# A fused attention, gate and embedding layer: where the last sums and reloads stand at the seam into the gate product

## The chip, the cores and the metric

The kernel runs on one core of a Trainium2 chip. The metric is the device time of one execution in microseconds (us), here the median of several runs. All times below that are not called runs come from one profiled execution.

## The reference

One layer, for a sequence of 1024 positions and a width of 1024, all in float32:

```python
h = rms_norm(x, mix_norm_g)
dq, dk, dv, bq, bk, bv, z = split(h @ w_in)
A = diff_attention(...)      # 4 heads, difference of two softmaxes, ALiBi, norm of each head
B = dilated_attention(...)   # 8 heads, three window patterns merged by their denominators
x = x + (concat[A, B] * silu(z)) @ w_out
gate = sigmoid(rms_norm(x, ple_norm_g) @ w_ple_gate)
x = x + gate * (p @ w_ple_proj)
```

## The kernel before

Everything is computed transposed, with features on the 128 partitions. Each float32 operand of a large product is cut into a rounded part "hi" and a rest "lo": ScalarE (ACT) casts the hi part, VectorE (DVE) or GpSimd (POOL) subtracts it to get the lo part, and TensorE (PE) does three matmuls (hi·hi, hi·lo, lo·hi) for each block of 128 features. Unless said otherwise a tile is 128x512.

The program has stages that follow each other on PE: the first projections, the dilated attention, the differential attention with the z product woven in, the product with `w_o`, and at the end the product with the gate weights `w_g` and the embedding. Two seams matter here.

**Seam 1, the end of the differential attention** (`step(g)`, g from 30 to 35). For each pair of query blocks `values` accumulates in a PSUM tile `od`, ACT squares it, and `sums` adds the squares over the partitions with four small matmuls into a PSUM tile `pss`, which DVE copies to `ssq` (L1202). `od` and `pss` are made in the same PSUM pool. `factors(3, 0, 4, V)` turns the first four sums of the last head into scale factors: a chain of small 128x4 instructions on DVE (tiles `dtmp`, `dfac`: L104, L106, then three rounds of L113, L115, L117, then L1237). It is a generator, and `bit(n)` issues the next n of its pieces where `step` calls it. `z_part(n)` issues the next n matmuls of the z and `w_o` products (`pso`), which fill PE between the parts of the attention.

**Seam 2, from the `w_o` product into the gate product.** The gate product of two feature blocks at once uses seven products of sums and differences (a Strassen-Winograd scheme): with the four quarters of `x1` (11, 21, 22 and a sum) and three more sums t2, t3, t4 of them on one side, and the weights' quarters with their sums s1, s2, s4 on the other. `sums_x1(3)` makes the last t2, t3, t4 on DVE (tiles `xe`, `xd`), each cut into hi and lo (`bt`). `w_gate(i)` loads the weights of step i, makes their sums on POOL and cuts all seven; step 0's are made ahead, those of step i+1 within step i. In the loop over i, `m(ps, w, k)` is one of the seven products (12 matmuls), and `taken` copies a PSUM tile to SBUF on ACT (L1624): `p1`, `p5`, `u2`, `u3`. The products "22", "t2", "t3" and "t4" accumulate into PSUM tiles that have been copied before, so each of them waits for such a copy. `norm2` sums the squares of `x1` with 16 matmuls of one column (tile `pm`) and ends in a broadcast reload `rb2`. `emb_product` is the embedding's product (6 matmuls, PSUM tile `psp`), from weights `wpr` and inputs `p` that `emb_w` and `emb_in` load and cut. `out_gate` scales, takes the sigmoid through tanh, multiplies, adds `x1` (reloaded from HBM by `x1_in` on ACT's DMA queue) and stores.

In seam 1 the order on PE, DVE, ACT, POOL and SP is the order of the code. From the end of the first `w_o` blocks on (`MAN4 = "PG"`) it is so for PE and POOL alone; DVE, ACT and SP follow a scheduler's list. Every engine works through its own list in order, and a DMA issue that waits for a buffer holds what stands behind it on its queue, on ACT the compute too.

Of the kernel before, what the change touches and what calls it, by code (L numbers as in the profile page):

```python
# [18 lines left out]
P = 128  # L19
# [55 lines left out]
def tile_hybrid_layer(ctx: ExitStack, tc, xT, w_att, w_z, w_o, w_g, w_p, pT, vec, lamv, tdil, tdiff, outT):  # L75
# [704 lines left out]
    with ExitStack() as pb:  # L780
# [528 lines left out]
        def step(g):  # L1309
            k = g // 2  # L1310
            zp_ = ZP[0], ZP[1] + (g % 3 == 0)
            if g >= 31:
                zp_ = ZT[g - 31]
            in_slot()
            scores(g + 1, 0)
            bit(BITS)
            z_part(zp_[0])
            exps(g + 1, 0)
            combine(g)
            bit(BITS)  # L1320
            turn(g - 1, 0)
            turn(g - 1, 1)
            if g % 2:
                sums(k - 2)
                if g in (11, 19, 27):
                    small_ops.append(factors((g - 11) // 8))
                elif g == 31:
                    small_ops.append(factors(3, 0, 4, V))
                elif g == 35:
                    for _ in factors(3, 4, 8, V):  # L1330
                        pass
            scores(g + 1, 1)
            turn_lo(g - 1, 0)
            turn_lo(g - 1, 1)
            if g < 32:
                bit(BITS)
            if g % 2:
                if 26 < g < 32:
                    z_part(zp_[1])
                values(k - 1, 0)  # L1340
            else:
                values(k - 2, 1)
            if g > 31:
                in_slot()
                bit(BITS)
            bit(BITS)
            if g < 32:
                fetch(g)
            if g % 2 == 0 or not 26 < g < 32:
                z_part(zp_[1])  # L1350
            if g in Y_IN:
                y_diff_in(*Y_IN[g])
            if g - 1 in Y_IN:
                y_diff(*Y_IN[g - 1])
            if g in (32, 33):
                y_split(6, g - 32, ga[2, g - 32][0])
            if g == 33:
                bit(100)
                G.tensor_mul(heads["a"][:, 0:512], heads["a"][:, 0:512], last_z[0])
            if g == 34:  # L1360
                y_last(0)
            bit(BITS)
            exps(g + 1, 1)
# [20 lines left out]
    with ExitStack() as pc:  # L1384
# [15 lines left out]
        def p_tile(shape, name):  # L1400
            return ps_t.tile(shape, F32, tag="t", name=name)

        def stage(name, src, q=nc.sync):
            t = inp.tile([P, 512], F32, tag="in", bufs=4, name=name)
            q.dma_start(t, src)
            return t
# [76 lines left out]

        def sums_x1(i):

            e, d = X[2 * i, "e"], X[2 * i, "d"]
            V.scalar_tensor_tensor(out=e, in0=X[2 * i + 1, 1], scalar=g2(2 * i + 1), in1=e, op0=ALU.mult, op1=ALU.subtract)
            V.scalar_tensor_tensor(out=d, in0=X[2 * i, 0], scalar=g2(2 * i), in1=e, op0=ALU.mult, op1=ALU.add)
            cut("t2", i, d)
            cut("t3", i, e)  # L1490
            V.scalar_tensor_tensor(out=d, in0=X[2 * i + 1, 0], scalar=g2(2 * i + 1), in1=d, op0=ALU.mult, op1=ALU.subtract)
            cut("t4", i, d)
# [42 lines left out]
        def emb_w(n):  # L1535
            hi, lo = wp[n] = [h_tile(f"wp{k}_{n}").rearrange("p (f a c) -> p f a c", f=4, a=2) for k in ("hi", "lo")]
            for b in range(2):
                fs = slice(2 * b, 2 * b + 2)
                raw = stage(f"wpr_{n}_{b}", w_p[n][:, fs].rearrange("p f a c -> p (f a c)"))
                split(hi[:, fs], lo[:, fs], raw.rearrange("p (f a c) -> p f a c", f=2, a=2))  # L1540
# [10 lines left out]
        def w_gate(i):  # L1551
# [9 lines left out]
            t = {1: q11, 5: s1, 2: q12, 6: s2, 7: q21, 3: s4, 4: q22}  # L1561
            return {n: w_cut(t[n], f"m{n}_{i}", G if i == 1 and n in (1, 5, 6) else V) for n in ORDER[i > 0]}

# [4 lines left out]
        out(7, 1)  # L1568
        sums_x1(3)
        first = h_tile("p15").bitcast(F32)  # L1570
# [24 lines left out]
        def g_tile(name):  # L1595
            return gp.tile([P, 512], F32, tag="g", bufs=6, name=name)

        pls = {}

# [14 lines left out]
        def x1_in(f, half):  # L1614
            t = gp.tile([P, 512], F32, tag="x", bufs=2, name=f"x1b_{f}_{half}")
            A.dma_start(t, x1_d[f, :, half * 512 : half * 512 + 512])
            return t
# [11 lines left out]
        for i in range(4):  # L1629
# [6 lines left out]
            first = []  # L1636
            if after:
                after.pop(0)()
            if i == 0:
# [3 lines left out]
                V.tensor_add(p1, p1, pb_)  # L1643
                m(pc_, w[3], "22", **more)
                emb_w(0)
                emb_in(0)
                emb_in(1)
                w_next = w_gate(1)
            m(pa_, w[6], "t2", **more)
            u2 = taken(f"u2_{i}", pa_)  # L1650
            if i:
                m(pb_, w[2], "21")
                V.tensor_add(p1, p1, pb_)
# [16 lines left out]
            else:  # L1670
                m(pa_, w[7], "t3", **more)
            u3 = taken(f"u3_{i}", pa_)
            if i == 0:
                emb_product(f0, 1)
                out_gate(f0, 0, p1, p1, x1_in(f0, 0))
                out_gate(f0, 1, u2, u2, x1_in(f0, 1))
            elif i < 3:
                w_next = w_gate(i + 1)
            G.tensor_add(u3, u3, p5)

# [106 lines left out]
```

## Time and profile before

| what | us |
|---|---|
| median of 3 runs (825.5 to 828.95) | 825.77 |
| the profiled execution's own time | 826.21 |
| its span, first to last instruction | 824.4 |
| PE busy in the span | 804.6 |
| DVE busy | 594.4 |
| ACT busy | 484.7 |
| POOL busy | 393.0 |
| mean granted clock of PE | 0.993 of full |

A granted clock of 1.00 is PE's upper level, 2.4 GHz; 0.50 is its lower level, 1.2 GHz. A matmul's row gives its start and a duration that runs into the next one's, so the pace of a stretch is read from the starts.

### The profile page before, as it was taken

How to read it: one execution, taken by the hardware profiler on the slowest of the kernel's cores; microseconds unless marked ns; L12 is line 12 of the kernel's file. 1: busy time of each engine (PE TensorE's matmuls, PEld its weight loads, DVE VectorE, ACT ScalarE, POOL GpSimd, SP SyncE). 2: the span in 40 equal slices, each digit the busy share in tenths (PEclk: the TensorE clock that was granted, in tenths of full speed). 3: DMA queues.
4: the chain of work that ended last, by engine and by line, in shares of the span. 5: the costliest groups of instructions: out<-in, count | busy, mean ns of one | idle time of the engine just before them, and what ended most of it. 6: DMA issues, size and time to landing. Idle time of an engine off the chain costs nothing.

```text
span 824.4 us, 13381 instructions
## 1 busy us (share of the span) xinstructions
PE 804.6 (98%) x4328; PEld 685.1 (83%) x4328; DVE 594.4 (72%) x1307; ACT 484.7 (59%) x1000; POOL 393.0 (48%) x432
## 2 busy tenths in 40 slices
PE   9999999999999999999999999999999999989997
PEld 8888888888788888887788888888887888868886
DVE  6948544566977687765788787888864598776773
ACT  8553423366866696665687877886771355443331
POOL 5602110226672665122367898885562343744552
PEclk9999999999999999999999999999999999989999
DMA  7621679465878579897487683944591453443422
GB/s 270 203 65 52 187 218 305 156 158 141 239 214 243 136 244 270 250 271 199 131 227 192 180 256 116 268 128 161 191 401 40 158 175 102 154 142 130 137 81 98
DMA packets 114773, 150.22 MB, mean 182 GB/s; under 512 B 11264, under 2 KB 70288, under 8 KB 114704
## 3 DMA queue, kind: packets, MB, share of 16 engines
q1 hardware_dynamic: 111680, 144.00, 57.7%
q10 hardware_dynamic: 3024, 5.38, 2.1%
q8 instruction: 34, 0.56, 0.3%
q14 instruction: 35, 0.29, 0.1%
HBM read 101.95 MB, written 47.39 MB: 181 GB/s over the span
## 4 chain that ended last, share of the span: by engine, by line
PE 80%; DVE 8%; issue 4%; POOL 4%; ACT 3%; DMA 1%; DVEq 0%; ACTq 0%; POOLq 0%
PE mm L256 5%; PE mm L258 5%; PE mm L257 5%; PE mm L508 5%; PE mm L512 5%; PE mm L510 5%; PE s L598 3%; PE psz L960 2%; PE psz L962 2%; PE psz L958 2%; PE sd L1114 2%; PE pso L1430 2%; PE pso L1428 2%; PE pso L1429 2%; PE sd L1115 2%
## 5 line engine op out<-in xcount | busy, mean ns | idle before, releaser
L1138 POOL TENSOR_TENSOR ed<-ed,ed 128x512 f32<-128x512 f32 x64 | 81.6, 1298 | 49.7 <-ACT ed L1136 44.3
L1126 ACT ACTIVATE ed<-ed,nm 128x1024 f32<-128x1024 f32 x64 | 73.8, 1153 | 47.0 <-DVE nm L1117 47.0
L627 ACT ACTIVATE e<-e,stats 128x256 f32<-128x256 f32 x128 | 64.8, 508 | 33.9 <-DVE stats L618 33.4
L510 PE MATMUL mm<-w2l,h_hi 128*128 128x512 f32 x192 | 78.9, 411 | 0.0
L508 PE MATMUL mm<-w2h,h_hi 128*128 128x512 f32 x192 | 78.6, 409 | 0.0
L512 PE MATMUL mm<-w2h,h_lo 128*128 128x512 f32 x192 | 76.0, 396 | 0.0
L257 PE MATMUL mm<-wl,h_hi 128*128 128x512 f32 x192 | 75.3, 392 | 0.0
L258 PE MATMUL mm<-wh,h_lo 128*128 128x512 f32 x192 | 75.1, 391 | 0.0
L256 PE MATMUL mm<-wh,h_hi 128*128 128x512 f32 x192 | 74.1, 392 | 0.0
L618 DVE CUSTOM_DVE_ANT_0 e<-s,tb 128x256 f32<-128x256 f32 x128 | 49.0, 418 | 20.3 <-PE s L598 19.6
L656 DVE TENSOR_TENSOR pl<-t,ph 128x512 fp32r<-128x512 f32 (+2 forms) x72 | 45.2, 628 | 19.1 <-ACT ph L651 17.0
L1117 DVE CUSTOM_DVE_ANT_0 ed<-sd,td,nm 128x512 f32<-128x512 f32 x64 | 48.1, 751 | 11.0 <-PE sd L1115 1.5
L1117 DVE CUSTOM_DVE_ANT_0 ed<-sd,td 128x512 f32<-128x512 f32 x64 | 43.9, 686 | 16.6 <-PE sd L1115 15.4
L1114 PE MATMUL sd<-kh,qs 128*128 128x512 f32 x128 | 53.4, 417 | 1.1 <-DVE nm L1117 0.6
L651 ACT CAST ph<-t 128x512 fp32r<-128x512 f32 (+2 forms) x72 | 38.2, 532 | 23.3 <-PE t L638 11.5
L1159 DVE TENSOR_TENSOR pld<-td,phd 128x512 fp32r<-128x512 f32 x64 | 42.0, 687 | 12.5 <-ACT phd L1150 12.1
L1115 PE MATMUL sd<-kl,qs 128*128 128x512 f32 x128 | 50.1, 392 | 0.0
L958 PE MATMUL psz<-h_hi,zhi 128*128 128x512 f32 x128 | 50.1, 392 | 0.0
L960 PE MATMUL psz<-h_lo,zhi 128*128 128x512 f32 x128 | 50.1, 392 | 0.0
L962 PE MATMUL psz<-h_hi,zlo 128*128 128x512 f32 x128 | 50.1, 391 | 0.0
L432 POOL TENSOR_TENSOR sq<-raw 128x512 f32<-128x512 f32 x16 | 17.1, 1070 | 63.4 <-ACT raw L430 61.1
L257 PEld LDWEIGHTS mm<-wl,h_hi 128*128 128x128 f32 x192 | 36.1, 188 | 7.4
(341 smaller groups left out, 2491.6 us busy)
## 6 DMA issues: line engine op xcount, KB each, us to landing
kn<-bk_d SPq DMA_DIRECT2D x16, 512.0 KB, 7.6
w2r<-in_w_att_dram SPq DMA_DIRECT2D x24, 256.0 KB, 4.3
y<-yd_d SPq DMA_DIRECT2D x12, 512.0 KB, 7.3
x<-in_xT_dram SPq DMA_DIRECT2D x16, 256.0 KB, 5.4
wr<-in_w_att_dram SPq DMA_DIRECT2D x8, 512.0 KB, 4.6
qn<-bq_d SPq DMA_DIRECT2D x16, 256.0 KB, 5.1
bv_d<-bv SPq DMA_DIRECT2D x16, 256.0 KB, 4.1
vc<-bv_d SPq DMA_DIRECT2D x32, 128.0 KB, 4.4
```

Source lines behind the costliest of these rows:

```text
L256: T.matmul(ps, h_hi[d][:, ts_], wh, start=(d == 0), stop=False)
L257: T.matmul(ps, h_hi[d][:, ts_], wl, start=False, stop=False)
L258: T.matmul(ps, h_lo[d][:, ts_], wh, start=False, stop=(d == 7))
L508: T.matmul(ps, h_hi[d][:, ts_], wh, start=(d == 0), stop=False)
L510: T.matmul(ps, h_hi[d][:, ts_], wl, start=False, stop=False)
L512: T.matmul(ps, h_lo[d][:, ts_], wh, start=False, stop=(d == 7))
L958: T.matmul(ps, hi, h_hi[d][:, hs], start=(d == 0), stop=False)
L960: T.matmul(ps, hi, h_lo[d][:, hs], start=False, stop=False)
L1114: T.matmul(ps, q, kh[:, c, hs], start=True, stop=False)
L1117: V.tensor_tensor_reduce(out=sp[:, hs], in0=ps, in1=td[:, off : off + 512], scale=4.0 ** -(hd + 1), scalar=BIG if half == 0 else nm[:, 0:1 ...
L1126: A.activation(sp, sp, AF.Exp, bias=nm[:, 1:2], scale=-1.0, accum_out=l)
L1138: G.tensor_add(w[:, hs], w[:, hs], e1[:, hs])
```

## The change

`step` no longer issues pieces of the factors' chain from g = 32 on; the remaining ones all come at g = 33, behind the copy of the row sums. At g = 33 three of the second half's z-path matmuls are taken ahead of `values`. In seam 2 the third sum of `sums_x1(3)` (t4) is split off as `sum_t4` and issued after "22". `w_gate(1)` is called behind `u3`'s copy and the sum `u3 + p5`; in the later steps that sum moves ahead of `w_gate(i + 1)`. The lo cuts of `w_gate(1)`'s products 1, 5 and 6 go from POOL to DVE. The reloads of `x1` use the four "in" buffers except for the first feature block, and the second embedding weights use the two "x" buffers. The postponed second embedding product of step 0 and the last one of each later step move one product on.

```diff
-            bit(BITS)
+            n_bits = BITS if g < 32 else 0
+            bit(n_bits)
...
                 sums(k - 2)
+                if g == 33:
+                    bit(10)
...
             if g % 2:
-                if 26 < g < 32:
-                    z_part(zp_[1])
+                if 26 < g < 34:
+                    z_part(zp_[1] if g < 32 else 3)
                 values(k - 1, 0)
...
-                z_part(zp_[1])
+                z_part(zp_[1] - 3 * (g == 33))
...
-        def sums_x1(i):
+        def sums_x1(i, late=False):
...
+            if not late:
+                sum_t4(i)
+
+        def sum_t4(i):
+            d = X[2 * i, "d"]
             V.scalar_tensor_tensor(out=d, in0=X[2 * i + 1, 0], scalar=g2(2 * i + 1), in1=d, op0=ALU.mult, op1=ALU.subtract)
             cut("t4", i, d)
...
-                raw = stage(f"wpr_{n}_{b}", w_p[n][:, fs].rearrange("p f a c -> p (f a c)"))
+                raw = (x_tile if n else in_tile)(f"wpr_{n}_{b}")
+                nc.sync.dma_start(raw, w_p[n][:, fs].rearrange("p f a c -> p (f a c)"))
...
-            return {n: w_cut(t[n], f"m{n}_{i}", G if i == 1 and n in (1, 5, 6) else V) for n in ORDER[i > 0]}
+            return {n: w_cut(t[n], f"m{n}_{i}") for n in ORDER[i > 0]}
...
-        sums_x1(3)
+        sums_x1(3, late=True)
...
-            t = gp.tile([P, 512], F32, tag="x", bufs=2, name=f"x1b_{f}_{half}")
+            t = (in_tile if f else x_tile)(f"x1b_{f}_{half}")
...
-            if after:
-                after.pop(0)()
...
                 m(pc_, w[3], "22", **more)
+                sum_t4(3)
                 emb_w(0)
                 emb_in(0)
                 emb_in(1)
-                w_next = w_gate(1)
...
             if i:
+                if len(after) > 1:
+                    after.pop(0)()
                 m(pb_, w[2], "21")
...
             u3 = taken(f"u3_{i}", pa_)
+            G.tensor_add(u3, u3, p5)
             if i == 0:
+                w_next = w_gate(1)
...
-            G.tensor_add(u3, u3, p5)
```

On DVE at seam 1 the chain of factors stands, before the change, ahead of the copy of the row sums (`ssq_6896<-pss`) and partly ahead of the cuts `pld` and the product `asb`:

```order
L113 TENSOR_TENSOR dtmp_0_7702<-dfac_0_7701 128x4
L115 SCALAR_TENSOR_TENSOR dtmp_0_7702<-dtmp_0_7702,sub_6897 128x4
L1159 TENSOR_TENSOR pld_0_7655<-td_0_7721,phd_0_7654 128x4x128
L1159 TENSOR_TENSOR pld_1_7663<-td_1_7727,phd_1_7662 128x4x128
L1185 TENSOR_TENSOR asb_7422<-od_7686,zt_1_7633 128x256
L117 SCALAR_TENSOR_TENSOR dfac_0_7701<-dtmp_0_7702,dfac_0_7701 128x4
L113 TENSOR_TENSOR dtmp_0_7702<-dfac_0_7701 128x4
L115 SCALAR_TENSOR_TENSOR dtmp_0_7702<-dtmp_0_7702,sub_6897 128x4
L117 SCALAR_TENSOR_TENSOR dfac_0_7701<-dtmp_0_7702,dfac_0_7701 128x4
L1270 TENSOR_TENSOR y_0_7762<-ya_0_7538,y_0_7762 128x512
L1237 TENSOR_SCALAR dfac_0_7701<-dfac_0_7701 128x4
L1202 COPY ssq_6896<-pss_7778 128x2
```

and after it:

```order
L113 TENSOR_TENSOR dtmp_0_7702<-dfac_0_7701 128x4
L1159 TENSOR_TENSOR pld_0_7655<-td_0_7717,phd_0_7654 128x4x128
L1159 TENSOR_TENSOR pld_1_7663<-td_1_7723,phd_1_7662 128x4x128
L1185 TENSOR_TENSOR asb_7422<-od_7686,zt_1_7633 128x256
L1270 TENSOR_TENSOR y_0_7754<-ya_0_7538,y_0_7754 128x512
L1202 COPY ssq_6896<-pss_7769 128x2
L115 SCALAR_TENSOR_TENSOR dtmp_0_7702<-dtmp_0_7702,sub_6897 128x4
L117 SCALAR_TENSOR_TENSOR dfac_0_7701<-dtmp_0_7702,dfac_0_7701 128x4
```

The copy L1202 now stands behind two cuts, one product and the cut of y alone; the rest of the chain follows it.

On ACT at seam 2, before the change, the copies of `psa` and `psc` (tile `p15`) stand behind the cast of the last sum, `bt4`:

```order
L1449 CAST bt3_3_8601<-xe_6_8555 128x512
L138 CAST whi_m4_0_8516<-wr_g011_8481 128x512
L1449 CAST bt4_3_8605<-xd_6_8550 128x512
L1624 COPY p15_8608<-psa_0_8614 128x512
L1624 COPY p15_8608<-psc_0_8616 128x512
L138 CAST wphi_0_8692<-wpr_0_0_8694 128x512
```

and after it they stand ahead of that cast; further down, the copy `u2` stands behind the reloads `x1b` of four more tiles:

```order
L1453 CAST bt3_3_8601<-xe_6_8555 128x512
L1637 COPY p15_8604<-psa_0_8610 128x512
L138 CAST whi_m4_0_8516<-wr_g011_8481 128x512
L1637 COPY p15_8604<-psc_0_8612 128x512
L1453 CAST bt4_3_8689<-xd_6_8550 128x512
...
L1409 DMA p_1_1_8717<-in_pT_dram 128x512
L1629 DMA x1b_1_0_8831<-x1_d_7910 128x512
L1557 ACTIVATE emb_1_0_8714<-p_1_0_8712 128x512
L1629 DMA x1b_1_1_8897<-x1_d_7910 128x512
L1557 ACTIVATE emb_1_1_8719<-p_1_1_8717 128x512
L1629 DMA x1b_2_0_8946<-x1_d_7910 128x512
L1629 DMA x1b_2_1_8973<-x1_d_7910 128x512
L1637 COPY u2_0_8734<-psa_0_8610 128x512
```

The line numbers differ by the change alone (L1624 is L1637 after it, L1449 is L1453). Both copies of `p15` moved ahead of `bt4`, and `u2` moved behind the reloads and ahead of the casts of the next weights.

On POOL, before the change, the four sums of step 1's weights (`wr_s1_1` to `wr_s4_1`) and three lo cuts stand right behind the last sum of `acc`:

```order
L1482 TENSOR_TENSOR acc_7933<-acc_7933,sq_7_1_8593 128x512
L1557 TENSOR_TENSOR wr_s_1_8730<-wr_g_8724,wr_g_8726 128x512
L1558 TENSOR_TENSOR wr_s_1_8731<-wr_s_1_8730,wr_g_8722 128x512
L1559 TENSOR_TENSOR wr_g_8724<-wr_g_8722,wr_g_8724 128x512
L1560 TENSOR_TENSOR wr_s_1_8732<-wr_g_8728,wr_s_1_8731 128x512
L140 TENSOR_TENSOR wlo_m_1_8738<-wr_g_8722,whi_m_1_8737 128x512
```

and after it the sum `u3 + p5` stands between:

```order
L1486 TENSOR_TENSOR acc_7933<-acc_7933,sq_7_1_8593 128x512
L1686 TENSOR_TENSOR u_0_8763<-u_0_8763,p_8604 128x512
L1567 TENSOR_TENSOR wr_s_1_8774<-wr_g_8768,wr_g_8770 128x512
L1568 TENSOR_TENSOR wr_s_1_8775<-wr_s_1_8774,wr_g_8766 128x512
L1569 TENSOR_TENSOR wr_g_8768<-wr_g_8766,wr_g_8768 128x512
L1570 TENSOR_TENSOR wr_s_1_8776<-wr_g_8772,wr_s_1_8775 128x512
```

POOL's four sums now wait for `u3`'s copy, which comes after the product "t3"; the three lo cuts are gone from POOL.

## Rows read from the trace of the kernel before

In rows of a timeline the columns are start (us from the span's start), duration in us, engine, line, operation, output<-input, shapes, count, and in brackets the engine's idle time before the row with what ended it.

**Rows 1.** The page's first part: busy time, share of the span and instructions of each engine.

```profile
PE 804.6 (98%) x4328; PEld 685.1 (83%) x4328; DVE 594.4 (72%) x1307; ACT 484.7 (59%) x1000; POOL 393.0 (48%) x432
```

**Rows 2.** The view of waits, PE, whole span, its two longest: what waited, for whom, us in total, times, longest.

```profile
PE psc L1428 <- ACT p L1624: 3.3, 1, 3.3
PE od L1173 <- DVE ssq L1202: 2.4, 2, 1.8
```

**Rows 3.** Busy time by engine in one stretch, from the second seam to just ahead of the end: stretch, its length, then busy us and count for PE, PE's weight loads, DVE, ACT, POOL, then the granted clock, the DMA engines' busy share and GB/s.

```profile
736.00:819.00 83.00, 83.00 (x379) 69.05 (x377) 52.95 (x63) 26.86 (x47) 35.19 (x24) 1.00 0.34 115
```

**Rows 4.** Timeline of PE at seam 1, and ahead of it a group of 12 `od` matmuls at full pace.

```profile
616.47 0.28 PE L1173 MATMUL od<-phd,vd 128*128 128x256 f32 x1
...
617.90 0.60 PE L1245 MATMUL pfac<-ident,dfac 128*128 128x128 f32 x4
...
624.77 0.58 PE L1201 MATMUL pss<-ones,sqd 128*128 128x1 f32 x4
627.12 0.39 PE L1173 MATMUL od<-phd,vd 128*128 128x256 f32 x1 [1.77 <-DVE ssq L1202]
...
631.58 0.39 PE L1027 MATMUL pso<-y,zhi 128*128 128x512 f32 x1
```

**Rows 5.** Busy time by engine, as in rows 3, in two stretches of seam 1 and two of seam 2.

```profile
624.77:627.12 2.35, 0.58 (x6) 0.50 (x5) 2.26 (x7) 0.00 (x0) 1.14 (x1) 1.00 0.00 0
627.12:631.58 4.46, 4.46 (x18) 3.93 (x19) 0.54 (x1) 0.00 (x0) 0.00 (x0) 0.62 0.00 0
722.70:726.00 3.30, 0.01 (x2) 0.01 (x1) 3.22 (x4) 1.65 (x4) 2.02 (x2) 0.62 0.00 0
726.00:730.86 4.86, 4.86 (x13) 3.84 (x13) 4.59 (x11) 2.66 (x6) 2.47 (x2) 0.55 0.69 215
```

**Rows 6.** Timeline of DVE at seam 1: one link of the chain, the cuts `pld`, the copy of the row sums.

```profile
621.09 1.28 DVE L113 TENSOR_TENSOR dtmp<-dfac 128x4 f32<-128x4 f32 x1
...
623.08 1.28 DVE L1159 TENSOR_TENSOR pld<-td,phd 128x512 fp32r<-128x512 f32 x2
...
626.91 0.15 DVE L1202 COPY ssq<-pss 128x2 f32<-128x2 f32 x1
```

**Rows 7.** Timeline of PE at seam 2: the first matmuls of "11" and "t1", the 16 sums of squares, the first matmul of "22" and of "t3".

```profile
712.70 0.39 PE L1428 MATMUL psa<-b,whi_m 128*128 128x512 f32 x1
...
715.42 0.39 PE L1428 MATMUL psc<-bt,whi_m 128*128 128x512 f32 x1
...
720.86 1.84 PE L1579 MATMUL pm<-ones,acc 128*128 128x1 f32 x16
726.00 0.80 PE L1428 MATMUL psc<-b,whi_m 128*128 128x512 f32 x1 [3.29 <-ACT p L1624]
...
735.65 0.50 PE L1428 MATMUL psa<-bt,whi_m 128*128 128x512 f32 x1 [0.54 <-ACT u L1624]
```

**Rows 8.** Timeline of ACT and its DMA queue (ACTq) at seam 2: the cast of `bt4`, the copy of `psc`, the last load of `p`, its cast, the copy `u2`.

```profile
724.35 0.62 ACT L1449 CAST bt<-xd 128x512 fp32r<-128x512 f32 x1 [3.06 <-DVE xd L1491]
...
725.35 0.59 ACT L1624 COPY p<-psc 128x512 f32<-128x512 f32 x1
...
728.09 0.34 ACTq L1405 DMA_DIRECT2D p<-in_pT_dram  x1
...
731.79 0.63 ACT L1547 ACTIVATE emb<-p 128x512 fp32r<-128x512 f32 x1
...
735.01 0.58 ACT L1624 COPY u<-psa 128x512 f32<-128x512 f32 x1
```

**Rows 9.** Timelines of DVE and, in the last row, of POOL at seam 2: the first and last of the sums of `x1`, the cut of `bt4`, the second cut of `wpr`; one of POOL's sums.

```profile
715.46 1.78 DVE L1487 SCALAR_TENSOR_TENSOR xe<-x,vec_sb,xe 128x512 f32<-128x512 f32 x1
...
722.57 1.75 DVE L1491 SCALAR_TENSOR_TENSOR xd<-x,vec_sb,xd 128x512 f32<-128x512 f32 x1
...
725.00 0.69 DVE L1450 TENSOR_TENSOR bt<-xd,bt 128x512 fp32r<-128x512 f32 x1
...
727.38 0.68 DVE L140 TENSOR_TENSOR wplo<-wpr,wphi 128x512 fp32r<-128x512 f32 x1
...
722.06 1.71 POOL L1559 TENSOR_TENSOR wr_g<-wr_g,wr_g 128x512 f32<-128x512 f32 x1
```

**Rows 10.** Busy time by engine, as in rows 3, in the stretch in which the two first reloads of `x1` and the two last loads of `p` move.

```profile
727.00:731.00 4.00, 4.00 (x12) 3.16 (x11) 3.93 (x10) 1.80 (x4) 1.63 (x1) 0.58 0.81 254
```

**Rows 11.** Timelines of ACT, POOL, DVE and PE around the end of step 1's "t3" and the start of step 2's "t1": `u3`'s copy, the first of the four sums of the weights, the lo cuts of two of them, the first matmul of "t1".

```profile
764.70 0.59 ACT L1624 COPY u<-psa 128x512 f32<-128x512 f32 x1
...
762.63 1.29 POOL L1557 TENSOR_TENSOR wr_s<-wr_g,wr_g 128x512 f32<-128x512 f32 x1
...
765.78 3.48 DVE L140 TENSOR_TENSOR wlo_m<-wr_s,whi_m 128x512 fp32r<-128x512 f32 x2
...
771.30 0.39 PE L1428 MATMUL psc<-bt,whi_m 128*128 128x512 f32 x1
```

**Rows 12.** PE elsewhere: a wait of 1.09 us in the dilated attention and the stretch around it; then the stretch that follows 16 one-column matmuls of the first norm (form as in rows 3).

```profile
381.16 0.35 PE L686 MATMUL o<-ph,vc 128*128 128x256 f32 x1 [1.09 <-ACT ph L651]
...
382.00:384.00 2.00, 2.00 (x12) 1.75 (x13) 1.81 (x4) 1.68 (x4) 1.33 (x2) 1.00 0.64 125
...
56.40:60.00 3.60, 3.60 (x18) 2.95 (x18) 3.19 (x11) 2.96 (x6) 0.00 (x0) 1.00 0.00 0
```

**Rows 13.** Timeline of ACT: the copy `u2` of step 1, behind the issue of a reload of `x1`.

```profile
754.32 0.59 ACT L1624 COPY u<-psa 128x512 f32<-128x512 f32 x1 [2.67 <-DVE u L1611]
```

More of the change, by code (lines that the diff above doesn't have):

```diff
@@ L1319, in step @@
             combine(g)
-            bit(BITS)
+            bit(n_bits)
             turn(g - 1, 0)
@@ L1334, in step @@
             turn_lo(g - 1, 1)
-            if g < 32:
-                bit(BITS)
+            bit(n_bits)
             if g % 2:
-                if 26 < g < 32:
-                    z_part(zp_[1])
+                if 26 < g < 34:
+                    z_part(zp_[1] if g < 32 else 3)
                 values(k - 1, 0)
@@ L1344, in step @@
                 in_slot()
-                bit(BITS)
-            bit(BITS)
+            bit(n_bits)
             if g < 32:
@@ L1361, in step @@
                 y_last(0)
-            bit(BITS)
+            bit(n_bits)
             exps(g + 1, 1)
@@ L1401, in p_tile, with in_tile @@
             return ps_t.tile(shape, F32, tag="t", name=name)
+        def in_tile(name):
+            return inp.tile([P, 512], F32, tag="in", bufs=4, name=name)
         def stage(name, src, q=nc.sync):
-            t = inp.tile([P, 512], F32, tag="in", bufs=4, name=name)
+            t = in_tile(name)
             q.dma_start(t, src)
@@ L1596, in g_tile, with x_tile @@
             return gp.tile([P, 512], F32, tag="g", bufs=6, name=name)
+        def x_tile(name):
+            return gp.tile([P, 512], F32, tag="x", bufs=2, name=name)
         pls = {}
```

## The prediction

> **What bounds the kernel now.** I read the page's busy times first: PE is busy for 98% of the span [rows 1], so only PE's own gaps and its clock are left to win here, and a gap of another engine counts only where PE waits for it. Second, the view of waits for PE: its two longest entries are 3.3 us for ACT's copy `p`, and 2.4 us in two waits for DVE's copy `ssq`, the longer of 1.8 us [rows 2]. Third, the timeline of PE at those two waits, with the granted clock of the stretches behind them. The reader is to see that each gap costs twice. At seam 1 PE idles 1.77 us, and the matmuls that follow run at a granted 0.62; at seam 2 it idles 3.29 us, with 0.62 during the gap and 0.55 behind it [rows 4, 5, 7]. In these stretches PE spent part of the time at its lower level, 1.2 GHz. Fourth, the last 83 us: PE is busy in all of them at 1.00 [rows 3], so a microsecond won at seam 2 arrives at the end whole, unless the change makes a new wait there.
>
> **Seam 1.** Today the row sums' matmuls `pss` start at 624.77, the copy `ssq` runs only at 626.91, and `od` starts at 627.12 [rows 4, 6]. The copy is late because DVE works in order and the factors' chain stands ahead of it; one 128x4 link alone takes 1.28 us while POOL works. After the change only the cuts `pld`, the product `asb` and one cut of `y` stand between the chain's first round and the copy. The first L113 ends at 622.37, the two cuts take 1.28 [rows 6], and the other two at most the 0.69 of a full-size cut each [rows 9], so DVE is free at 625.0 at the latest. The copy then follows `pss`, which ends at 625.35, and is through at 625.5. Meanwhile PE does the three `pso` matmuls moved ahead of `od`, to about 626.0, so `od` finds its buffer free.
>
> The sum: from 624.77 to 631.58 PE takes 6.81 us today [rows 4]. The work in it is `pss` 0.58, 12 `od` at the pace of the earlier group (617.90 - 616.47 = 1.43 [rows 4]), and 6 `pso` at the pace of "11" (12 matmuls in 715.42 - 712.70 = 2.72 [rows 7], 0.227 each) = 1.36. Together 3.37, so 3.44 us go. The rest of the chain, some ten small instructions, now runs behind the copy: 2 to 3 us, costed at nothing because the factors are used by `pfac` several us later, with the `w_o` matmuls of the second half between; if that cover is gone, PE waits for `pfac`, at most those 3 us. Lower bound of the gain 1.8 (the gap alone returns and the clock falls anyway for another reason), upper 3.7 (`pss` without its drain).
>
> **Seam 2, the copies.** "22" accumulates into `psc` and may start when `p5` is copied. That copy ends at 725.94, since ACT stands in `bt4`'s cast, which waited for DVE's last sum, L1491 [rows 8, 9]. After the change both copies stand ahead of `bt4`. They follow `bt3`'s cast and need PE's "t1" alone, long finished, so they are done before the 16 matmuls `pm` end at 722.70 [rows 7]; "22" follows `pm` without a gap.
>
> **Seam 2, DVE.** `w_gate(1)`'s sums leave POOL's place behind `acc`. A DVE instruction beside a POOL sum takes 1.75 to 1.78, without one 0.69 [rows 9]. From the end of L1487 at 717.24 DVE has two cuts, `xd`, two more cuts and L1491 to do, at about 0.6 to 0.7 from start to start: L1491 ends near 721.2, not 724.32; `bt4` is cut by 722.6, not 725.69; the embedding weights' second cut ends near 724.4, not 728.06 [rows 9]. The rest is 3.1 to 3.7 us earlier, so "t2" and `psp` find their operands. The three lo cuts that come to DVE from POOL cost 0.69 each, one here (counted), two behind the critical part.
>
> **Seam 2, what is late next.** "t3" needs the copy `u2`; today that is a wait of 0.54 [rows 7]. In ACT's new order four reloads of `x1` stand ahead of it, the last of which takes the buffer of the last load of `p`, and so waits until DVE has cut it. That load was issued at 728.09, right behind the cut that ended at 728.06 and freed its buffer; its cast ran at 731.79, 3.70 later [rows 8, 9]. From 724.45 the cast comes at 728.15 and ends at 728.8; the cut takes 0.69, to 729.5; the reload's issue about 0.4; the copy 0.58 [rows 8], to 730.5. "t3" starts at 730.6. Without the wait PE would be there after 30 matmuls (722.70 + 30 x 0.227 = 729.5), so a gap of 1.1 us stays. Does the clock fall behind it? After a gap of 1.09 us elsewhere the granted clock was 1.00, and also behind 16 one-column matmuls like `pm` [rows 12]; I say no. The gain is 735.65 - 730.6 = 5.05. Bounds: 6.15 if the copy is not late at all (735.65 - 729.5), and about 2.2 if it is a further microsecond late and the clock falls.
>
> One figure here can be weighed. In 727 to 731 the queues moved 254 GB/s, about 1.02 MB, which is just the four transfers of 256 KB then under way [rows 10]: two reloads and two loads of `p`. After the change these four are issued within 1.4 us, not 2.4. The Trainium skill, "DMA: Bandwidth & Descriptors", section "Issuing engines are not separate DMA queues", says that transfers from all issuing engines end on the same 16 DMA engines and interleave. By that rule the last load lands with the sum of the four, which would put the copy some 0.3 us later (estimate) and the gain at 4.75; the trace agrees as far as its share of 0.81 goes.
>
> **Seam 2, the moved sums and buffers.** POOL's four sums now wait for `u3`. From the end of "t3" to the first use of their first result, "t1" of the next step, lie 771.30 - 764.65 = 6.65 us [rows 11]. The new chain is `u3`'s copy 0.59, the sum 1.29, the first weight sum 1.29, the cast 0.62 [rows 8, 11]: 3.8, then the lo cut, at most 1.75 beside POOL, which is needed two matmuls later. 2.8 us are left for the cast and 1.5 for the cut, in all three steps, so this costs nothing. Today's order has those cuts done by 769.3. On SP, `rb2`'s reload stands ahead of the next weights' loads and not behind three of them, and the second embedding weights come after the first outputs; both are used many products later. The moved `psp` products find a PSUM buffer freed at least one product before.
>
> **The sum.** 3.44 + 5.05 = 8.5 us. The profiled execution took 826.21, 0.44 above the median of 825.77, a difference that concerns neither seam. 826.21 - 8.5 = 817.7 in the profile's own terms, 817.3 against the median, 1.0% less.
>
> **Rivals.**
> - *The reloads hold ACT.* For: in step 1 today `u2`'s copy stood 2.67 us behind a reload that waited for DVE [rows 13]; the four reloads now stand ahead of the copy that PE needs first. If the last `p` lands 1 us later, the gap grows to 2.1, above the 1.77 that was followed by the lower level at seam 1 [rows 4, 5]. The price is 1 us and about 2.0 us of slow matmuls (ten at 0.43 and not 0.227, as 726.00 to 730.86 shows [rows 5]): 820.3. Against: DVE is no longer held by POOL there.
> - *The weights are late.* If ACT is held once more ahead of the cast of step i+1's second product, the slack of 1.5 to 2.8 is used up and "t1" waits about 0.8 us in each of three steps: 819.7. Against: the buffers those reloads wait for are freed before "t3" ends [rows 11].
> - *One seam doesn't close*, because another engine ends the wait at the same time (ACT's square or a load of `y` at seam 1, the cut of t2 or `emb` at seam 2): 820.7 with seam 1 alone failing, 822.4 with seam 2 alone. Against: each such operand was there well before today's wait ended.
> - *Slower.* The same late weights, with the clock: a wait behind "11" as long as seam 1's 1.77 us would put PE on the lower level as it did there, and each of three steps then costs the wait and about 2.0. Against a gain of 8.5 it is slower than before from 3 x (w + 2.0) > 8.5, w over 0.83 us if the clock falls that early; with w = 2.5, 13.5 - 8.5 = 5 more, 830.8. It needs a chain of 9.1 us where I count 3.8: two holds of 2.67 each, three times.
> - *It does nothing*: the scheduler's order on the chip ends in the same waits, 825.8.
>
> **Chances and range.** Forecast 0.64 (815.7 to 819), reloads hold ACT 0.14, late weights 0.08, one seam open 0.06, nothing 0.05, slower 0.03. The best case is 3.7 + 6.15 off 825.77, 815.9; with 0.2 for the spread of the runs the range starts at 815.7. At the top it takes in the first two rivals and the seam-1 case with 0.5 for the spread: 821.2. What a measurement of this kernel can tell from no change is about 0.5%, 4.1 us, so faster means below 821.6: the forecast, two rivals and half of the third, 0.89. Within 0.5%: 0.08. Slower: 0.03.
>
> **What would show it.** In the profile after: no PE wait for `ssq` at seam 1 and 1.00 behind it; the first matmul of "22" directly behind `pm`; a PE wait of 0.7 to 1.6 us for `u2`'s copy and 1.00 behind it; no other wait of PE to the end. L1491 (L1500 after) at 0.75 and not 1.75. It is wrong if PE waits at "t1" of steps 1 to 3 for the casts, if the granted clock is below 1.00 behind `u2`'s wait, or if `pfac` of the last head waits for the factors' chain.

## The result and the profile after

The kernel takes 818.39 us after the change (median of 6 runs, 817.33 to 820.04), against 826.27 before (6 runs on the same chip): ratio 0.990, 95% interval 0.988 to 0.992. The profiled execution took 819.4, with a span of 817.6 and a mean granted clock of 0.999. Of the 6.8 us by which the span is shorter, 3.0 are idle time of PE (824.4 - 804.6 before, 817.6 - 800.8 after); the other 3.8 are busy time, matmuls that no longer run at the lower clock.

The page's first part after the change, one row; it answers to [rows 1].

```profile
PE 800.8 (98%) x4328; PEld 682.2 (83%) x4328; DVE 591.4 (72%) x1310; ACT 485.3 (59%) x1000; POOL 389.6 (48%) x429
```

PE's waits over the whole span after the change, as in [rows 2].

```profile
PE psa L1432 <- ACT u L1637: 1.4, 1, 1.4
...
PE t L648 <- DVE lo L474: 0.7, 1, 0.7
PE od L1173 <- DVE ssq L1202: 0.6, 1, 0.6
...
PE psp L1432 <- DVE p L1623: 0.4, 1, 0.4
```

The wait of 3.3 for `p` is gone, and of the two for `ssq` only the earlier one is left. In their place stand 1.4 us for `u2`'s copy, where 0.5 stood, and, new, 0.4 us of an embedding product for a PSUM buffer. The wait at L648 lies near 380 us, in code that the change doesn't touch.

PE at seam 1, to set beside [rows 4]: the row sums, the three matmuls taken ahead, the first `od`, the seventh `pso`.

```profile
625.39 0.50 PE L1201 MATMUL pss<-ones,sqd 128*128 128x1 f32 x4
625.75 0.49 PE L1027 MATMUL pso<-y,zhi 128*128 128x512 f32 x1
...
626.54 0.28 PE L1173 MATMUL od<-phd,vd 128*128 128x256 f32 x1
...
628.67 0.40 PE L1027 MATMUL pso<-y,zhi 128*128 128x512 f32 x1
```

No row has a bracket: PE does not wait. From `pss` to the seventh `pso` it takes 628.67 - 625.39 = 3.28 us, where it took 6.81.

PE at seam 2, to set beside [rows 7]: the 16 sums of squares, the first matmul of "22", of "t3", and, in step 1, the last matmul ahead of the postponed embedding product, that product's first, and the first of "21" behind it.

```profile
717.94 1.84 PE L1589 MATMUL pm<-ones,acc 128*128 128x1 f32 x16
719.64 0.49 PE L1432 MATMUL psc<-b,whi_m 128*128 128x512 f32 x1
...
728.15 0.50 PE L1432 MATMUL psa<-bt,whi_m 128*128 128x512 f32 x1 [1.41 <-ACT u L1637]
...
743.16 0.39 PE L1434 MATMUL psa<-bt,wlo_m 128*128 128x512 f32 x1
743.92 0.50 PE L1432 MATMUL psp<-emb,wphi 128*128 128x512 f32 x1 [0.38 <-DVE p L1623]
...
745.42 0.39 PE L1432 MATMUL psb<-b,whi_m 128*128 128x512 f32 x1
```

Busy time by engine after the change, in the form of [rows 3]: seam 1, seam 2 up to the gap, the gap, and the 3.85 us behind it. The clock is 1.00 in all four, where [rows 5] had 0.55 and 0.62.

```profile
625.39:628.67 3.28, 3.28 (x23) 3.01 (x22) 2.94 (x12) 0.00 (x0) 1.61 (x1) 1.00 0.00 0
...
717.94:726.80 8.86, 8.80 (x47) 7.23 (x45) 7.02 (x17) 4.88 (x9) 0.00 (x0) 1.00 0.53 176
...
726.80:728.15 1.35, 0.00 (x0) 0.00 (x0) 1.18 (x8) 0.59 (x1) 0.00 (x0) 1.00 0.45 135
728.15:732.00 3.85, 3.85 (x17) 3.11 (x18) 0.95 (x2) 0.59 (x1) 0.00 (x0) 1.00 0.28 96
```

ACT and its queue after the change, to set beside [rows 8]: the copy of `psc`, the last load of `p` and its cast, two reloads, the copy `u2`.

```profile
717.73 0.59 ACT L1637 COPY p<-psc 128x512 f32<-128x512 f32 x1
...
721.51 0.34 ACTq L1409 DMA_DIRECT2D p<-in_pT_dram  x1
...
725.67 0.63 ACT L1557 ACTIVATE emb<-p 128x512 fp32r<-128x512 f32 x1
726.41 1.00 ACTq L1629 DMA_DIRECT2D x1b<-x_d  x2
727.51 0.59 ACT L1637 COPY u<-psa 128x512 f32<-128x512 f32 x1 [1.21 <-DVE mst L115]
```

DVE after the change, and in the last row POOL, to set beside [rows 9]: the last sum of `x1`; then, in step 1, the two cuts that came from POOL, two further cuts and the product that frees the PSUM buffer; two products of `out_gate` on POOL.

```profile
717.55 0.75 DVE L1500 SCALAR_TENSOR_TENSOR xd<-x,vec_sb,xd 128x512 f32<-128x512 f32 x1
...
735.23 2.93 DVE L140 TENSOR_TENSOR wlo_m<-wr_s,whi_m 128x512 fp32r<-128x512 f32 x2 [5.00 <-ACT whi_m L138]
...
740.00 1.56 DVE L140 TENSOR_TENSOR wlo_m<-wr_s,whi_m 128x512 fp32r<-128x512 f32 x1
741.49 1.79 DVE L140 TENSOR_TENSOR wlo_m<-wr_g,whi_m 128x512 fp32r<-128x512 f32 x1
743.20 0.67 DVE L1623 SCALAR_TENSOR_TENSOR p<-p,psp 128x512 f32<-128x512 f32 x1
...
740.97 3.43 POOL L1621 TENSOR_TENSOR u<-u,rb 128x512 f32<-128x512 f32 x2
```

The last sum takes 0.75 us where it took 1.75 beside POOL. The stretching itself is not gone: it now falls on cuts of step 1, beside POOL's four sums (733.25 to 739.31) and the products that follow them (739.27 to 744.40).

### The profile page after: what moved, and what is told of

Read it like the earlier page. It is cut to its first block, busy times and chain, and to the rows that moved or that the text cites. A ratio compares the mean times of both kernels' runs of the same rounds, so it can differ in the third digit from the quotient of the medians.

```text
span 817.6 us, 13372 instructions
## 1 busy us (share of the span) xinstructions
PE 800.8 (98%) x4328; PEld 682.2 (83%) x4328; DVE 591.4 (72%) x1310; ACT 485.3 (59%) x1000; POOL 389.6 (48%) x429
## 4 chain that ended last, share of the span: by engine, by line
PE 77%; DVE 8%; issue 7%; POOL 3%; ACT 3%; DMA 2%; SPq 0%; DVEq 0%; POOLq 0%; ACTq 0%
PE mm L256 5%; PE mm L258 5%; PE mm L257 5%; PE mm L508 5%; PE mm L512 5%; PE mm L510 5%; PE s L598 3%; PE pso L1434 2%; PE pso L1433 2%; PE pso L1432 2%; PE psz L962 2%; PE psz L960 2%; PE sd L1114 2%; PE psz L958 2%; PE o L698 2%
```

## The experiments

Twelve kernels were run. The first table gives each against the kernel before on its own chip; e13 is the changed kernel itself once more.

| kernel | median us (runs) | ratio to before, 95% |
|---|---|---|
| changed | 818.39 (6) | 0.990, 0.988 to 0.992 |
| e13 changed again | 819.37 (5) | 0.992, 0.991 to 0.994 |
| e1 seam 2 alone | 821.63 (7) | 0.993, 0.991 to 0.996 |
| e2 seam 1 alone | 824.19 (12) | 0.997, 0.996 to 0.999 |
| e3 sums early | 825.33 (12) | 0.998, 0.997 to 1.000 |
| e4 t4 early | 819.18 (6) | 0.990, 0.988 to 0.993 |
| e8 buffers as before | 819.54 (6) | 0.992, 0.990 to 0.994 |
| e11 sums late alone | 826.83 (14) | 1.000, 0.999 to 1.001 |
| e5 reloads on SP | 818.53 (6) | 0.992, 0.989 to 0.994 |
| e12 t4 early, reloads on SP | 818.93 (5) | 0.991, 0.990 to 0.993 |
| e6 psp later | 824.72 (12) | 0.998, 0.997 to 1.000 |
| e9 t4 early, psp later | 824.09 (12) | 0.998, 0.996 to 0.999 |
| e10 pop early | 822.89 (9) | 0.996, 0.995 to 0.998 |

The second table cuts each profiled span at three starts on PE: the `pss` at seam 1, `pm`, and the first matmul of "t3". Between them PE's work is fixed, so a wait shows here to 0.1 us that the medians can't resolve; but each row is one execution.

| kernel | start to `pss` | `pss` to `pm` | `pm` to "t3" | "t3" to end |
|---|---|---|---|---|
| before | 624.8 | 96.09 | 14.79 | 88.75 |
| changed | 625.4 | 92.55 | 10.21 | 89.45 |
| e13 | 625.7 | 92.55 | 9.79 | 89.51 |
| e1 | 626.1 | 96.01 | 9.66 | 89.46 |
| e2 | 625.6 | 92.55 | 14.94 | 88.80 |
| e3 | 625.6 | 92.55 | 15.03 | 90.46 |
| e4 | 624.2 | 92.55 | 10.53 | 89.25 |
| e8 | 624.5 | 92.54 | 10.23 | 89.98 |
| e11 | 629.9 | 96.00 | 14.66 | 88.85 |
| e5 | 626.1 | 92.54 | 8.65 | 89.34 |
| e12 | 625.2 | 92.55 | 10.55 | 89.33 |
| e6 | 624.1 | 92.54 | 9.74 | 95.11 |
| e9 | 629.3 | 92.55 | 10.26 | 92.49 |
| e10 | 625.8 | 92.55 | 10.06 | 93.65 |

**Each seam alone (e1, e2).** The changed kernel with the old `step`, and the kernel before with the new one:

```diff
-            n_bits = BITS if g < 32 else 0
-            bit(n_bits)
+            bit(BITS)
...
-                if g == 33:
-                    bit(10)
...
```

> The changed kernel with the attention's step as it was before (the last factors' chain back ahead of the row sums' copy); seam 2 as changed. Theory A, each seam closed for itself: the gap at `od` comes back (2.4 us in all waits of od L1173, 1.8 of them at the seam) with the slower clock behind it, and the time is that of the changed kernel plus the 3.53 us that its seam 1 gained, 818.4 + 3.5 = 821.9. Rival B, the two seams share the gain (time won at seam 1 is lost again in a later wait): at most 1.5 us above the changed kernel, below 819.9. Rival C, seam 1 also carried seam 2: over 823.5.

> The kernel before with only the attention's step as changed; seam 2 as before. Theory A, each seam for itself: the wait for ssq at the seam goes, pss to the seventh pso takes about 3.3 us rather than 6.81, seam 2 keeps its gaps of 3.3 us (psc) and 0.5 (psa), and the time is that of before less 3.5, 826.3 - 3.5 = 822.8. Rival B, the gain is lost again in a wait that comes later (the slow stretch at seam 2 grows): above 824.5. Rival C, the earlier seam helps seam 2 too: below 821.

Theory A holds. The stretch `pss` to `pm` is 96.0 with the old step and 92.55 with the new one in every kernel, so seam 1 is worth 3.5 us whatever stands behind it. e1's 821.63 is as expected. e2's median is 1.4 above its number, and by ratio its gain lies between 0.7 and 3.6 us, an interval that just takes in the 3.5. Its stretches decide: against the kernel before, `pss` to `pm` is 3.54 shorter, and the two behind it differ by 0.15 and 0.05; the first, 0.8 longer, has the same work on PE. The gains by ratio, 5.5 us (0.0066 of 826.66) and 2.2, add to 7.7; the changed kernel gains 8.3 and 6.4 in its two sets. Which of seam 1's two edits carries how much was not tried. By the trace after, the copy of the row sums ends at 626.09; without the three matmuls ahead of it, `od` would be asked at 625.75, so some 0.4 us of wait would be left (estimate from these rows).

**Which part closes seam 2 (e3, e4, e8, e11).** e3 puts the weights' sums back, e4 the sum of t4, e8 the buffers, each in the changed kernel; e11 makes the sums late in the kernel before.

```diff
                 emb_in(1)
+                w_next = w_gate(1)
...
-                w_next = w_gate(1)
```

> The changed kernel with w_gate(1) back at its old place in step 0 (behind emb_in), its cuts of 1, 5 and 6 on POOL again; the last sum of x1 stays behind the first copies. Theory P, the place of the copies closes the gap: 22 still follows pm without a wait, POOL's sums beside DVE only lengthen cuts that nothing waits for, and since these sums no longer lie beside step 1 the wait of 0.38 us of psp for DVE's p goes: 818.4 with at most 0.5 to either side. Theory Q, POOL away from DVE closes the gap: DVE's instructions from 712 to 727 us take 1.75 us rather than 0.7 again, 22 or t3 waits 1 to 3 us longer and the clock falls with it: 820.0 to 822.5. Theory R, either part is enough: as P.

In e3 "22" follows `pm` without a wait, as P says, and yet `pm` to "t3" takes 15.03 us, more than before. PE's waits behind 700 us in e3:

```profile
PE psa L1432 <- ACT u L1637: 4.6, 1, 4.6
PE psp L1433 <- DVE emb L1558: 1.3, 1, 1.3
```

DVE in e3, with one of POOL's sums:

```profile
719.31 1.73 POOL L1569 TENSOR_TENSOR wr_g<-wr_g,wr_g 128x512 f32<-128x512 f32 x1
719.82 1.77 DVE L1500 SCALAR_TENSOR_TENSOR xd<-x,vec_sb,xd 128x512 f32<-128x512 f32 x1
...
723.49 2.89 DVE L140 TENSOR_TENSOR wplo<-wpr,wphi 128x512 fp32r<-128x512 f32 x2
```

ACT and its queue in e3:

```profile
724.71 2.04 ACTq L1409 DMA_DIRECT2D p<-in_pT_dram  x2
...
730.18 0.63 ACT L1557 ACTIVATE emb<-p 128x512 fp32r<-128x512 f32 x1 [0.85 <-DMA p<-in_pT_dram]
...
732.51 0.58 ACT L1637 COPY u<-psa 128x512 f32<-128x512 f32 x1
```

The gap ahead of "t3" and the matmuls behind it in e3, in the form of [rows 3]:

```profile
728.50:733.14 4.64, 0.04 (x1) 0.00 (x0) 3.17 (x9) 2.56 (x5) 1.73 (x2) 0.66 0.79 267
733.14:736.00 2.86, 2.86 (x8) 2.08 (x8) 0.69 (x1) 0.00 (x0) 0.82 (x1) 0.50 0.56 189
```

With POOL's sums beside it, DVE takes 1.77 for L1500 and 2.89 for the two cuts of `wpr` (1.28 after the change). So the buffers of `p` come free late and the last cast starts at 730.18; `u2`'s copy stands behind it, behind two reloads that end at 731.89 and behind a cast of step 1's weights. PE's next matmuls run at 0.50. The early copies closed the first gap; the time came back at the second. Neither P's time nor Q's came out: at 825.33 the loss is above Q's 822.5.

```diff
-        sums_x1(3, late=True)
+        sums_x1(3)
...
-                sum_t4(3)
```

> The changed kernel with the sum of t4 back ahead of the first copies (sums_x1(3) whole); POOL's sums stay late, reloads as changed. Theory P, the place of the copies closes the gap: p1 and p5 wait behind the cast of bt4, psc is taken late again, 22 waits 1 to 3 us for it and the clock falls: 820 to 822.5. Theory Q, POOL away from DVE closes it: with POOL silent L1491, L1492 and L1500 take 0.75 us each, the cast of bt4 ends about 717.8, both copies by 719.0, before pm ends at 719.8, and 22 follows pm without a wait: 818.4 with at most 0.4 to either side. Theory R, either part is enough: as Q.

In time Q and R hold: with POOL silent the copies may stand behind `bt4` again, and the total is the same within the interval, though 0.4 above their bound. But `pm` to "t3" is 10.53 with a single wait of 0.18 us, where 8.65 would do (`pm` and 30 matmuls without a wait, as in e5 below). PE in e4:

```profile
716.72 1.84 PE L1589 MATMUL pm<-ones,acc 128*128 128x1 f32 x16
718.73 0.50 PE L1432 MATMUL psc<-b,whi_m 128*128 128x512 f32 x1 [0.18 <-ACT p L1637]
```

The stretches of `pm` and of most of "22" in e4, in the form of [rows 3]:

```profile
716.72:718.73 2.01, 1.83 (x17) 1.75 (x15) 1.93 (x4) 1.64 (x4) 0.00 (x0) 1.00 0.00 0
718.73:722.00 3.27, 3.27 (x9) 2.56 (x10) 3.07 (x9) 2.55 (x5) 0.00 (x0) 0.56 0.57 205
```

The clock falls behind that wait: 10.53 - 8.65 - 0.18 = 1.7 us of slow matmuls. They also hide the wait for `u2`, since PE comes to "t3" that much later: in e9, which is e4 up to there and where the clock did not fall, "t3" waits 1.13 again and the stretch is 10.26. So in the changed kernel the late t4 saves nothing that shows, because `u2`'s copy ends the stretch either way.

e8 leaves all reloads in the two `x` buffers and both embedding weights in the four "in" buffers:

```diff
-            t = (in_tile if f else x_tile)(f"x1b_{f}_{half}")
+            t = x_tile(f"x1b_{f}_{half}")
```

> The changed kernel with the buffers of the reloads and of the second embedding weights as before (all reloads in the two x buffers, both weights in the four in buffers); the late sum of t4 and the late weights' sums stay. Theory F, the other buffers only free the reloads from one another: the copies of u2 is then no longer behind reloads (two casts of wphi stand there in their place, which wait for the weights), so t3 waits 0.2 to 2 us and the time is 817.5 to 819.5. Rival N, the buffers matter for the gain: the casts of wphi wait for their loads ahead of u2's copy as in the profile before, t3 waits over 3 us and the clock falls with it: 821 to 824.

Theory F: "t3" waits 1.42 us, as long as in the changed kernel, now with two casts of `wphi` ahead of `u2`'s copy (725.42 to 726.67) and not the reloads. The time, 819.54, lies at the edge of what F allowed. That part of the change moves nothing that can be measured.

e11 also has the cuts of 1, 5 and 6 on DVE:

```diff
-                w_next = w_gate(1)
...
             if i == 0:
+                w_next = w_gate(1)
                 emb_product(f0, 1)
```

> The kernel before with one part alone: the second weights' sums behind t3's copy and their cuts on DVE. Theory Q, POOL away from DVE closes the gaps at 22 and t3: the wait of psc goes from 3.29 to under 0.4 us and that of t3 stays under 1 us. By theory W (the postponed product asked behind t1 meets a DVE held by cuts) a wait of 2 to 4 us of psp then stands in step 1, and the time is about 826.3 - 4.6 + 3 = 824.5; without W it is 826.3 - 4.6 = 821.7, as the run with seam 2 alone. Rival P, the place of the copies closes the gap: psc still waits 2 us or more, 825 or above.

It did not do what it was made for. POOL and PE in e11:

```profile
721.66 1.74 POOL L1557 TENSOR_TENSOR wr_s<-wr_g,wr_g 128x512 f32<-128x512 f32 x1
725.35 1.77 POOL L1558 TENSOR_TENSOR wr_s<-wr_s,wr_g 128x512 f32<-128x512 f32 x1 [1.95 <-issue]
...
731.01 0.74 PE L1428 MATMUL psc<-b,whi_m 128*128 128x512 f32 x1 [3.28 <-ACT p L1624]
```

The first sum runs 4.2 us ahead of `pm` (725.89), as before the change (716.65 against 720.86). In POOL's list nothing stood between the sums and the last `acc`, so a later line in the code moved nothing there. In the change the sums are late because `u3 + p5` now stands ahead of them on POOL and waits for `u3`. With the sums where they were, neither theory was tried by this run; e3 and e4 carry that reading.

**The wait for `u2` (e5, e12, e13).** e5 issues the reloads of `x1` on SP's queue; e12 also has t4 early.

```diff
-            A.dma_start(t, x1_d[f, :, half * 512 : half * 512 + 512])
+            nc.sync.dma_start(t, x1_d[f, :, half * 512 : half * 512 + 512])
```

> The changed kernel with the reloads of x1 issued on SP's queue rather than on ACT's. Theory H, ACT is held by the reloads: two of them stand for 1.00 us between the last cast of emb and the copy of u2, so the wait of t3 for u2 falls from 1.41 to 0.2 to 0.4 us and the time by about 1.1 us, to 817.3. Rival L, the landing of the last loads of p alone sets it: the wait stays at 1.2 or more and the time at 818.4. Rival S, SP stands at a reload whose buffer is not free and the weights of the next steps come late: new waits for wr_g or wpr, 819.5 or more.

ACT in e5, from the last cast of `emb`:

```profile
725.89 0.63 ACT L1557 ACTIVATE emb<-p 128x512 fp32r<-128x512 f32 x1 [0.28 <-DMA p<-in_pT_dram]
726.43 0.57 ACT L1637 COPY u<-psa 128x512 f32<-128x512 f32 x1
```

Theory H: the copy follows the cast at once, "t3" does not wait, and `pm` to "t3" is 8.65, which is `pm` and 30 matmuls with nothing between. In the changed kernel the two reloads ahead of the copy take 1.00 us: 0.33 for each issue, and in the rest the second waits for DVE to free its buffer (the cut that ends at 727.06). They were the larger part of the 1.41 us; the last cast also comes 0.45 earlier behind `pm` in e5. The Trainium skill, "DMA: Bandwidth & Descriptors", section "Issuing engines are not separate DMA queues", says that spreading issues over engines saves only the sequencer's time, which is usually small beside the transfer. The trace agrees on the size, 0.33 us for an issue against 2.4 to 4.3 from issue to landing, but here just that time, and a wait for a buffer with it, stood ahead of a copy PE needed. The total, 818.53, can't tell the 1.1 to 1.6 us (9.79 and 10.21 less 8.65).

> The changed kernel with both edits that took the wait of t3 for u2 away: the sum of t4 ahead of the first copies and the reloads of x1 on SP's queue. By the waits (1.41 gone, 0.2 of psc new) the time is the changed kernel's less 1.2: 817.2, and below the changed kernel of this call by 0.5 to 1.5. Rival: waits of about 1 us at the full clock here are lost in what differs from execution to execution: within 0.5 of the changed kernel of this call.

> The changed kernel itself again, on the same chip as the other three of this call, as their measure: 818.4 with 0.7 to either side if the place of a run matters no more than the runs so far show.

e13, at 819.37, is 0.3 above the range that was expected of it, so sets of runs of one kernel differ by 1 us. e12 is 0.4 below e13, within the runs' spread, which is what its rival said, though not for its reason: in e12 the 0.18 us wait behind `pm` came back, and with it the slow clock. Here, with ACT free, the late t4 counts in the profiled executions: `pm` to "t3" is 8.65 with it (e5) and 10.55 without. The medians, 818.53 and 818.93, don't show it. No version was measurably faster than the changed kernel.

**The postponed embedding product (e6, e9, e10).** e6 asks it one product later than the change does, behind "21"; e9 is the same with t4 early; e10 asks it behind t1, where it stood before.

```diff
-                if len(after) > 1:
-                    after.pop(0)()
                 m(pb_, w[2], "21")
                 V.tensor_add(p1, p1, pb_)
+                if len(after) > 1:
+                    after.pop(0)()
```

> The changed kernel with the postponed embedding product of step 0 (f1, half 1) behind 21 of step 1 rather than ahead of it. Theory: psp waits 0.38 us for DVE's last read of its PSUM buffer (p at 743.20 us, late by the cuts beside POOL's sums); one product of 2.7 us later that buffer is free, the wait goes and with it 0.4 to 0.5 us: 818.0. Rival: the wait is passed on to what comes next (the following psp or 22), the time stays at 818.4 or rises by up to 0.5.

> The changed kernel with the sum of t4 back ahead of the first copies and the postponed embedding product behind 21 of step 1. In the run with t4 early alone the wait of t3 for u2 (1.4 us) was gone, with 0.2 for psc in its place and 0.4 for psp left. Theory: both small waits but 0.2 go, seam 2 is closed, the time is the changed kernel's less 1.2 and less 0.4, 816.8. Rival: what the profile's waits lose comes back elsewhere (the median with t4 early alone was 819.2 although its profiled execution took 818.4), no difference: 818 to 819.5.

> The changed kernel with the postponed embedding product of step 0 back at its old place in step 1, behind t1 (the next one behind t2), rather than behind t2 (and 21). Theory W, the wait for the PSUM buffer is set by DVE: psp waits for DVE's read of p, which stands behind cuts of 1.6 to 1.8 us beside POOL's sums; asked 2.7 us earlier, it waits 0.4 + 2.7 = 3.1 us, the clock falls behind it, and the time is 821 to 823. Rival N, DVE's order moves with it and the buffer is free in time: a wait under 1 us, 818 to 819.

e6's and e9's expectations fell. PE in e6:

```profile
750.65 0.79 PE L1432 MATMUL psp<-emb,wphi 128*128 128x512 f32 x1 [3.41 <-DVE u L1623]
```

DVE in e6:

```profile
748.71 0.69 DVE L140 TENSOR_TENSOR wplo<-wpr,wphi 128x512 fp32r<-128x512 f32 x1 [2.39 <-ACT wphi L138]
...
749.92 0.68 DVE L1623 SCALAR_TENSOR_TENSOR u<-u,psp 128x512 f32<-128x512 f32 x1
```

ACT in e6:

```profile
748.06 0.62 ACT L138 CAST wphi<-wpr 128x512 fp32r<-128x512 f32 x1 [1.67 <-DMA wpr<-in_w_p_dram]
```

The stretch behind the wait in e6, in the form of [rows 3]:

```profile
751.00:755.00 4.00, 4.00 (x10) 3.12 (x10) 3.93 (x6) 0.63 (x1) 0.35 (x1) 0.50 0.33 110
```

The wait of 0.38 went, but three embedding products now follow each other. The third needs a PSUM buffer that DVE frees only at 750.6, behind a cut that waits for ACT, which waits for a DMA. "t3" to the end grows by 5.7 us. In e9 the same product waits as long, and the stretch grows by 3.0 only, since there the clock stays at 1.00. PE in e9, and the stretch behind its wait:

```profile
756.36 0.50 PE L1432 MATMUL psp<-emb,wphi 128*128 128x512 f32 x1 [3.43 <-DVE u L1623]
...
756.36:760.00 3.64, 3.64 (x16) 3.03 (x17) 3.60 (x5) 0.63 (x1) 0.71 (x1) 1.00 0.22 54
```

Theory W holds for e10, though beside the two cuts ahead of DVE's read POOL runs two products of `out_gate`, no longer its sums. PE in e10:

```profile
744.17 0.79 PE L1432 MATMUL psp<-emb,wphi 128*128 128x512 f32 x1 [3.06 <-DVE p L1623]
```

The stretch behind that wait in e10:

```profile
745.00:750.00 5.00, 5.00 (x18) 3.94 (x18) 3.89 (x7) 0.31 (x1) 0.00 (x0) 0.75 0.51 154
```

3.06 us against the 3.1 expected, and 4.2 us more from "t3" to the end. The place that the change gives it, between t2 and 21, is the only one of the three at which PE waits under 1 us for such a buffer.

## Why the prediction was right, and where its steps were off

The forecast was 817.3, measured were 818.39 and 819.37. By the table of stretches the profile gained 3.54 and 4.58 and gave back 0.70 at the end, 7.4 us where 8.5 were counted: 0.47 went at `u2`'s copy and 0.70 at an embedding product, both below, and seam 1 gave 0.10 more. 0.6 more lay ahead of `pss`, where PE's work is the same.

- **Seam 1: right, one bound with luck.** 3.53 us against 3.44, no wait of `od`, clock 1.00. The copy of the row sums ran at 625.93, 0.54 behind the start of `pss`. DVE came to it some 0.2 us later than "at the latest": the cut of `y`, counted with 0.69, took 1.42 beside a POOL product of 1.74. It cost nothing because `pss` itself ended only then, at 625.89. The chain behind the copy cost nothing either: `pfac` did not wait.
- **Seam 2, the copies: right on the gap, wrong on its weight.** "22" follows `pm` directly. But e3 shows that the place alone is worth nothing in the end, and e4 that without it a wait of only 0.18 us is left. It pays only where nothing holds "t3" and the clock falls behind that wait (e5 against e12, one execution each).
- **Seam 2, DVE: right, and the part that carries.** Counted from `pm`, the last sum ended at +0.36 (717.55 + 0.75 - 717.94) where 721.2 meant +0.34. The first gap's other cause, the 1.75 us beside POOL, also held the second.
- **`u2`'s copy: the mechanism right, one term short.** By PE's starts "t3" came 10.21 us behind `pm` where 730.6 meant 9.74. The 0.47 is the load's: it was issued 3.57 us behind the start of `pm`, where 724.45 meant 3.59, and its cast came 4.16 later, not 3.70. Behind the cast all went as written: DVE's cut to 727.06, the reload's issue, the copy at 727.51. In e13 the cast came 3.77 later and the wait was 0.98. The estimate that the prediction took from the Trainium skill, "DMA: Bandwidth & Descriptors", section "Issuing engines are not separate DMA queues", meant 4.0; that lies between the two, so they decide neither for it nor against it. The four transfers were issued within 1.80 us, not 1.4. The clock stayed at 1.00, as [rows 12] led me to say.
- **The weights: right.** No wait at t1 in any of the three steps.
- **"The moved `psp` products find a PSUM buffer freed at least one product before": wrong.** It is freed too late: PE idles 0.38 us, and by the starts loses 0.67, since seven matmuls take 745.42 - 743.16 = 2.26 where 0.227 each makes 1.59. This is nearly all of the 0.70 that "t3" to the end was longer than before. DVE's read at 743.20 stands behind cuts of 1.56 and 1.79 us. They are not among the three that came from POOL: these are the cuts for "11" (0.68 at 721.39), "t1" and "t2", and the last two, counted as 0.69 each "behind the critical part", are the row at 735.23 with 2.93. The cuts ahead of the read DVE had to make before the change too; now they run beside POOL's two products of `out_gate`, which come behind the four moved sums. In e3, with the sums at their old place, `psp` does not wait for `p`. So the price that I had counted as won at seam 2 is in part paid in step 1.
- **The rivals** did not come. The nearest was the hold of ACT by the reloads: e5 shows the cause to be real; the clock stayed at 1.00 behind the wait. That this was for the wait's length, as the rival had it, is not shown: in e9 the clock stayed at 1.00 behind 3.43 us.

What stays open: whether e5 is faster in the total, how seam 1's gain divides between its two edits, and when the clock falls behind a wait and when not.

## What to carry to other kernels

Two engines that slow one another are worth parting where the path is tight, but follow the slowed instructions to where they go next: each stretched cut there may hold a buffer that another engine asks for. A line written later in the code moves nothing on an engine that has nothing ahead of it; put an instruction that waits in front. And where a change is worth a microsecond, compare stretches between fixed instructions in the profiles beside the medians, in more than one execution: e4 and e9 differ by the clock alone behind the same wait.

## What was not expected of the hardware

- **A wait of 0.18 us behind 16 one-column matmuls can cost 1.9 us.** In e4 and e12 the clock fell behind it (0.56 and 0.52 in the next 3.27 us); in e9, with the same wait, it did not, and in the executions where "22" follows `pm` at once it stayed at 1.00. Waits of 0.85 to 1.42 us ahead of "t3" left it at 1.00. Behind 3.41 us in e6 it was 0.50, behind 3.43 us in e9, at the same product, 1.00: the length of a wait alone did not decide it.
- **The same instructions start up to 5.8 us apart** (624.1 to 629.9 at `pss`) in executions in which PE's work up to there is the same. Most of it is one wait near 380 us and the clock behind it: under 0.3 us in the profile before, 0.7 after the change and, as this row of e9's waits shows, 2.7 there, with the clock at 0.86 from 378 to 390 us:

```profile
PE t L648 <- DVE lo L474: 2.7, 1, 2.7
```

- **DVE and POOL stretched each other at seam 1, at seam 2 and in step 1**: 0.69 to 1.42, 1.56 or 1.79 for a cut, 1.29 to 1.74 for a sum. The product at 743.20, with one input in PSUM, took 0.67 beside POOL. The Trainium skill, "SBUF — State Buffer", section "Who interferes with whom", says that a DVE instruction with both inputs in SBUF contends with POOL's reads; the cuts and sums here are of that form, and the trace agrees.
